# Scaling the odd token tiles by their norm on POOL instead of DVE in a decoder layer

## The chip, the cores and the metric

The kernel runs on one core of a Trainium2 chip. The metric is the device time of one execution in microseconds (us); the median of three runs of the kernel before is 1223.09 us (1221.67 to 1223.1). Engines are named as in the profile: PE multiplies matrices and transposes, DVE is the vector engine, ACT the scalar engine, POOL the general-purpose one (GpSimd), and SP only issues DMA transfers.

## The reference

One layer of a decoder: a pre-normed token mixer (sparse attention with three branches, beside a short gated convolution) and a squared-ReLU MLP, on 1024 tokens of width 1024. What matters here is its very first step:

```
def rms_norm(x, g):
    y = xf * lax.rsqrt(jnp.mean(xf * xf, axis=-1, keepdims=True) + EPS)
    return (y * g.astype(jnp.float32)).astype(x.dtype)
...
h = rms_norm(x, g_mix_norm[l])
z = h @ w_in[l]
```

`z` is then cut into queries, keys and values of the branches, gates and convolution channels. Everything behind it (compressed keys, attention, output projection, MLP) is left as it is by the change.

## The kernel before, in words

**Tiles.** The 1024 tokens are eight tiles `tb` of 128 (one token to a partition). `xts[tb]` (in the profile `xt`, 128x1024 f32) holds a tile. `norm_in(tb)` (line 632) normalizes it: ACT squares it into `junk` and sums into `ss` (line 636); `rsqrt` (line 556) multiplies and adds on DVE (`rs_t`) and raises to the power -1/2 on POOL (`ri`, 128x1); line 639 scales the whole tile in place by `ri`, one number to a token; then PE transposes it in two halves of four 128x128 blocks into a PSUM tile `tp` (line 644). `split_psum` (line 522) takes each half out of PSUM as a high part on ACT (`hTh`) and a rest on DVE (`hTl`); there are three PSUM buffers for `tp`. Tiles 0 to 3 go to `hTh0`/`hTl0`, tiles 4 to 7 to `hTh1`/`hTl1`.

**Products in three terms.** A product in f32 is made of three matmuls (`mm3`, line 526): high by high, high by rest, rest by high. Weights arrive in `w_raw` (two buffers to a shape), and `w_piece` (line 591) makes `w_hi` on ACT and `w_lo` on DVE, four pieces to a chunk of columns. `z_tokens` (line 664) multiplies four pieces with the transposed tokens into `zp`. The first chunk (lines 650 and 748) gives keys and values; `k_norm` and `v_split` finish them on ACT, DVE and POOL (`ksq`, `kri`, `krow`, `vrow`) and SP writes them to DRAM. The raw compressed-branch part goes to DRAM as `kv_d` and comes back as `ch` (line 771) for the compression, whose weights are the pieces `in_w_cmp1`.

**Sums.** `token_sums` (line 692) is a run of 128x512 additions and subtractions on DVE over `hTh` and `hTl` of all eight tiles (`ta`, `tb`, `t1`, `t2`, `t4`), needed later by a fast matrix multiplication.

**Two small loads on POOL's queue.** `gk_bc` and `gq_bc` (line 655), the norm weights of keys and queries spread over all partitions, are loaded by DMAs that POOL issues; one DVE multiplication (line 658) joins them.

**What sets the order.** The code does not run in the order it is written. `Plan` records every operation with what it needs, and `schedule` (line 340) orders them all: at each step the engine that is free first takes the ready operation of the highest priority, by fixed costs for each kind (`cost`, line 292). The resulting order of each engine is written into the program and does not change at run time: an engine that waits for an operand holds all that stands behind it in its row. Almost all operations carry line 268 in the profile, that of the recorder; tile names tell them apart.

Of the kernel before, what the change touches and what calls it, by code (L numbers as in the profile page):

```python
# [13 lines left out]
ALU = mybir.AluOpType  # L14
# [482 lines left out]
def trunk_layer(ctx, tc, x, g_mix_norm, w_in, g_q, g_k, pe_cmp, w_cmp1, b_cmp1, w_cmp2, b_cmp2,  # L497
                conv_w, g_out, w_o, g_ffn_norm, w_up, w_down, out):
    plan = Plan(tc)
    nc = plan.nc  # L500
# [6 lines left out]
    def pool(stack, name, bufs=1, side=None, space=None):  # L507
        kw = {}
        if side is not None:
            kw["side"] = side  # L510
        if space is not None:
            kw["space"] = space
        return stack.enter_context(plan.pool(name=name, bufs=bufs, reuse_waits="tile", **kw))


    def tt(eng, o, a, b, op):
        eng.tensor_tensor(o, a, b, op=op)
# [4 lines left out]
    def split_psum(hi, lo, ps):  # L522
        copy_act(hi, ps)
        tt(nc.vector, lo, ps, hi.bitcast(F32), ALU.subtract)
# [31 lines left out]
    def rsqrt(o, ss, n, scale):  # L556
        t = st.tile([P, n], F32, name="rs_t", tag=f"rs{n}")
        nc.vector.tensor_scalar(t, ss, scale, EPS, op0=ALU.mult, op1=ALU.add)
        nc.gpsimd.tensor_tensor(o, t, mhalf[:, :n], op=ALU.pow)
# [51 lines left out]
    def w_chunk(c0, n, lo_eng=None):  # L611
        return [w_piece(wiv[:, 2 * j:2 * j + 2, c0:c0 + n], [P, 2, n], gcol=G_MIX + 2 * j)
                for j in range(4)]


    with ExitStack() as a:
        xp = pool(a, "xp", bufs=2, side="right")
        xts = [xp.tile([P, D], F32, name="xt", tag="xt", bufs=8) for _ in range(NT)]
        plan.plus = 100.0
        nc.sync.dma_start(xts[0], x2d[0:P])  # L620
        plan.plus = 50.0
        rows = xp.tile([68, P], F32, name="rows", bufs=1)
        nc.sync.dma_start(rows[0:8], g_mix_norm.rearrange("l (k p) -> (l k) p", p=P))
        nc.sync.dma_start(rows[8:16], g_ffn_norm.rearrange("l (k p) -> (l k) p", p=P))
        nc.sync.dma_start(rows[16:24], g_out.rearrange("l (k p) -> (l k) p", p=P))
        nc.sync.dma_start(rows[24:36], conv_w.rearrange("j (k p) -> (j k) p", p=P))
        nc.sync.dma_start(rows[36:68], pe_cmp.rearrange("k (q two) d -> (k q) (two d)", two=2))
        plan.plus = 0.0
        tp = psP.tile([P, 512], F32, name="tp", tag="pt")
        nc.tensor.transpose(tp[:, :68], rows, ident[:68, :68])  # L630
        nc.vector.tensor_copy(cols, tp[:, :68])
        def norm_in(tb):
            xt = xts[tb]
            junk = xp.tile([P, D], BF16, name="junk", tag="junk", bufs=1)
            ss = st.tile([P, 1], F32, name="ss")
            nc.scalar.activation(junk, xt, AF.Square, accum_out=ss)
            ri = st.tile([P, 1], F32, name="ri")
            rsqrt(ri, ss, 1, 1.0 / D)
            nc.vector.tensor_scalar(xt, xt, ri, None, op0=ALU.mult)
            for half in range(2):  # L640
                tp = psP.tile([P, 4, P], F32, name="tp", tag="pt")
                for j in range(4):
                    k = half * 4 + j
                    nc.tensor.transpose(tp[:, j], xt[:, k * P:(k + 1) * P], ident)
                d = (slice(None), slice(half * 4, half * 4 + 4), slice((tb % 4) * P, (tb % 4 + 1) * P))
                split_psum(hTh[tb // 4][d], hTl[tb // 4][d], tp)

        nc.sync.dma_start(xts[1], x2d[P:2 * P])
        norm_in(0)
        kv_pieces = w_chunk(C_KV, 512)  # L650
        for tb in range(2, NT):
            last = nc.sync.dma_start(xts[tb], x2d[tb * P:(tb + 1) * P])
            if tb == 5:
                plan.follow = (last,)
                nc.gpsimd.dma_start(gq_bc, g_q.partition_broadcast(P))
                nc.gpsimd.dma_start(gk_bc, g_k.partition_broadcast(P))
                plan.follow = ()
                tt(nc.vector, gk_bc, gk_bc, gq_bc.unsqueeze(1).to_broadcast([P, 3, HD]), ALU.mult)
                plan.follow = ()
        for tb in range(1, NT):  # L660
            norm_in(tb)
# [60 lines left out]
    with ExitStack() as b1:  # L722
# [129 lines left out]
        for tb, ps in (a for tbs in (QUADS[1], (0,), (1,), (2,), (3,)) for a in z_tokens(pieces, tbs, 512, steps, 1)):  # L852
# [7 lines left out]
            ri = st.tile([P, H], F32, name="qri")  # L860
# [20 lines left out]
        for tb, ps in (a for tbs in (QUADS[1], (0, 1), (2,), (3,)) for a in z_tokens(pieces, tbs, 280)):  # L881
# [6 lines left out]
            for g in range(G):  # L888
                eg = e[:, g * 12:(g + 1) * 12].rearrange("p (i j b) -> p b j i", i=2, b=3)
                nc.vector.tensor_scalar(gates[:, tb, g].rearrange("p b (j i) -> p b j i", j=2), eg, 1.0, 1e20,  # L890
                                        op0=ALU.add, op1=ALU.min)
# [5 lines left out]
    with ExitStack() as b2:  # L897
# [150 lines left out]
        def y_tile(shape, name):  # L1048
            return yp.tile(shape, F32, name=name, tag="y", bufs=6)
# [167 lines left out]
        for it, tb in [*enumerate(ORDER)][6:] + [*enumerate(ORDER)][:6]:  # L1217
            xt = xq.tile([P, D], F32, name="xt") if it >= 6 else y_tile([P, D], f"y{tb}")
            nc.sync.dma_start(xt, x2d[tb * P:(tb + 1) * P])
            t = slice(tb * P, (tb + 1) * P)  # L1220
            for nh in range(2):
# [7 lines left out]
                for c in range(4):  # L1229
# [3 lines left out]
                                               op0=ALU.mult, op1=ALU.add)  # L1233
# [421 lines left out]
    for c in range(NPAIR // CHUNK):  # L1655
# [6 lines left out]
        for p in range(7):  # L1662
# [18 lines left out]
            for j in range(4):  # L1681
# [8 lines left out]
                tb = TH[ih] * 4 + j  # L1690
# [34 lines left out]
```

## Time and profile before

| what | value |
|---|---|
| median of 3 runs | 1223.09 us |
| time of the profiled execution | 1223.71 us |
| its span in the trace | 1221.9 us |
| PE busy in it | 1201.2 us (98%) |
| DVE busy | 918.9 us (75%) |
| ACT busy | 716.1 us (59%) |
| POOL busy | 709.3 us (58%) |
| granted TensorE clock | 1.00 |

The span runs from the first instruction to the last; the 1.8 us by which the execution's time is longer lies around it. Busy shares say how long an engine had an instruction running, not whether it set the pace: where PE issues one 128x512 matmul right behind the other, nothing that another engine does makes it faster. So the places to look at are those where PE waits, and what it waits for.

### The profile page before, as it was taken

The page shows a single profiled execution, that of the slowest core. Times are in us where ns is not written, and L with a number is a line of the kernel's source. Part 1 is how long each engine was busy: PE and PEld are TensorE (multiplying, and loading weights), DVE is VectorE, ACT ScalarE, POOL GpSimd, SP SyncE. Part 2 cuts the span into 40 slices and gives each one's busy share as a digit, 9 for nine tenths or more (in the row PEclk, how much of TensorE's full clock was granted, in tenths as well). Part 3 has the DMA queues.
Part 4 walks back from the last instruction along what each step waited for, and adds up shares of the span by engine and source line. Part 5 has one row for each costly group of instructions (what it writes and reads, how often), then busy time and mean ns, then how long its engine had stood idle before and what let it go on. Part 6 is the DMA issues. An engine that isn't in the chain of part 4 may idle for free.

```text
span 1221.9 us, 18330 instructions
## 1 busy us (share of the span) xinstructions
PE 1201.2 (98%) x5970; PEld 996.9 (82%) x5970; DVE 918.9 (75%) x1784; ACT 716.1 (59%) x1586; POOL 709.3 (58%) x629
## 2 busy tenths in 40 slices
PE   7999999999999999999999999999999999999998
PEld 6878978777878888888788888888888888888887
DVE  6958856684697889988876565656758988888885
ACT  7567855551588878787956555555445444444441
POOL 2544300011345444434759877777888999989971
PEclk9999999999999999999999999999999999999999
DMA  7275631155120101002225544445449545543513
GB/s 247 54 193 180 183 82 52 53 192 187 44 87 36 48 22 36 28 18 70 75 92 178 182 142 151 152 133 181 150 150 394 185 165 165 175 143 121 174 51 138
DMA packets 104215, 156.06 MB, mean 128 GB/s; under 512 B 20212, under 2 KB 58184, under 8 KB 104120
## 3 DMA queue, kind: packets, MB, share of 16 engines
q1 hardware_dynamic: 97976, 147.09, 36.6%
q10 hardware_dynamic: 5376, 5.24, 1.2%
q0 software_dynamic: 768, 2.56, 0.7%
q8 instruction: 47, 0.77, 0.3%
q14 instruction: 48, 0.39, 0.1%
HBM read 106.63 MB, written 48.23 MB: 127 GB/s over the span
## 4 chain that ended last, share of the span: by engine, by line
PE 87%; DVE 5%; ACT 2%; DMA 1%; issue 1%; POOL 1%; SPq 0%; ACTq 0%; DVEq 0%; POOLq 0%
PE X L268 28%; PE Z L268 18%; PE zX L268 5%; PE tp L268 5%; PE ot L268 4%; PE wa L268 4%; PE W L268 4%; PE zp L268 3%; PE wc L268 3%; PE zZ L268 3%; PE zW L268 1%; PE hp L268 1%; DVE w_lo L268 1%; DVE pl L268 1%; PE tpq L268 0%
## 5 line engine op out<-in xcount | busy, mean ns | idle before, releaser
L268 PE MATMUL X<-we,uu 128*128 128x512 f32 x720 | 202.3, 389 | 0.0
L268 PE MATMUL Z<-we,uu 128*128 128x512 f32 x576 | 169.1, 389 | 0.0
L268 PEld LDWEIGHTS X<-we,uu 128*128 128x128 f32 x720 | 135.1, 188 | 28.1
L268 ACT ACTIVATE uu<-ur 128x512 fp32r<-128x512 f32 x108 | 66.5, 630 | 118.9 <-PE Z L268 58.5
L268 PEld LDWEIGHTS Z<-we,uu 128*128 128x128 f32 x576 | 108.1, 188 | 22.5
L268 PE MATMUL tp<-ident,pt 128*128 128x128 f32 x528 | 103.6, 273 | 1.3 <-DVE pl L268 0.7
L268 ACT ACTIVATE pt<-pt,nm 128x640 f32<-128x640 f32 (+7 forms) x128 | 93.7, 735 | 18.9 <-DVE nm L268 18.3
L268 DVE TENSOR_TENSOR y<-X,y 128x512 f32<-128x512 f32 x128 | 86.4, 684 | 20.5 <-PE X L268 20.1
L268 POOL TENSOR_TENSOR d<-d 128x512 f32<-128x512 f32 x64 | 96.2, 1523 | 9.6 <-DVE d L268 7.5
L268 DVE TENSOR_TENSOR pl<-tp,ph 128x512 fp32r<-128x512 f32 (+1 forms) x148 | 94.6, 654 | 7.3 <-ACT ph L268 6.8
L268 ACT ACTIVATE ph<-tp 128x512 fp32r<-128x512 f32 (+1 forms) x148 | 82.2, 576 | 30.0 <-PE tp L268 27.9
L268 DVE TENSOR_TENSOR y<-Z,y 128x512 f32<-128x512 f32 x96 | 65.2, 685 | 27.3 <-PE Z L268 27.1
L268 POOL TENSOR_TENSOR uu<-ur,uu 128x512 fp32r<-128x512 f32 x54 | 82.2, 1527 | 1.1 <-ACT uu L268 0.9
L268 PEld LDWEIGHTS tp<-ident,pt 128*128 128x128 f32 x528 | 68.6, 140 | 14.0 <-POOL pt L268 1.0
L268 DVE TENSOR_TENSOR we<-s,we 128x512 fp32r<-128x512 f32 x42 | 41.1, 978 | 47.6 <-PE Z L268 19.0
L268 ACT ACTIVATE we<-s 128x512 fp32r<-128x512 f32 x55 | 34.7, 631 | 65.3 <-PE Z L268 36.7
L268 ACT ACTIVATE we<-wu 128x512 fp32r<-128x512 f32 x57 | 35.9, 631 | 54.7 <-PE X L268 37.4
L268 POOL TENSOR_TENSOR we<-wd,we 128x512 fp32r<-128x512 f32 x32 | 52.2, 1631 | 25.0 <-ACT we L268 24.5
L268 POOL IOTA d_sw<- 128x640 f32 (+1 forms) x2 | 1.2, 610 | 108.9 <-PE zZ L268 108.9
L268 DVE TENSOR_TENSOR we<-wu,we 128x512 fp32r<-128x512 f32 x38 | 49.5, 1304 | 19.2 <-PE X L268 9.8
L268 PE MATMUL zp<-w_lo,hTh 128*128 128x512 f32 (+1 forms) x192 | 62.2, 364 | 0.1
L268 PE MATMUL zp<-w_hi,hTl 128*128 128x512 f32 (+1 forms) x192 | 61.5, 363 | 0.0
(1334 smaller groups left out, 3733.4 us busy)
## 6 DMA issues: line engine op xcount, KB each, us to landing
u_d<-d SPq DMA_DIRECT2D x112, 256.0 KB, 4.4
ur<-u_d SPq DMA_DIRECT2D x108, 256.0 KB, 2.9
wu<-in_w_up_dram SPq DMA_DIRECT2D x16, 1024.0 KB, 6.2
wd<-in_w_down_dram SPq DMA_DIRECT2D x16, 1024.0 KB, 6.8
xt<-in_x_dram SPq DMA_DIRECT2D x10, 512.0 KB, 5.7
w_raw<-in_w_in_dram SPq DMA_DIRECT2D x8, 512.0 KB, 5.7
w_raw<-in_w_cmp_dram SPq DMA_DIRECT2D x16, 256.0 KB, 2.9
q_d<-qn SPq DMA_DIRECT2D x8, 512.0 KB, 3.5
```

What stands on the lines that cost most here:

```text
L268: node.do.append(lambda: getattr(engine, method)(*[real(x) for x in a], **{k: real(x) for k, x in kw.items()}))
```

## The change

Line 639 chooses the engine by the number of the tile. Tiles 0, 2, 4 and 6 are scaled on DVE as before; tiles 1, 3, 5 and 7 on POOL, behind the power that POOL has computed for that tile. The operation, its operands and its result are the same.

```
             ri = st.tile([P, 1], F32, name="ri")
             rsqrt(ri, ss, 1, 1.0 / D)
-            nc.vector.tensor_scalar(xt, xt, ri, None, op0=ALU.mult)
+            (nc.gpsimd if tb in (1,3,5,7) else nc.vector).tensor_scalar(xt, xt, ri, None, op0=ALU.mult)
             for half in range(2):
```

Since the order is made by the planner, other operations move too, on all engines, from the first token tiles to the end of the compression and the second weight chunk; behind that all rows are as before. Three places follow.

DVE in the first 30 us, before (`xt_165` to `xt_167` are tiles 5 to 7; `w_lo_133` and `w_lo_134` the third and fourth weight piece of the first chunk):

```order
L268 TENSOR_SCALAR rs_t_300<-ss_295 128x1
L268 TENSOR_SCALAR xt_165<-xt_165,ri_272 128x1024
L268 TENSOR_TENSOR hTl1_123<-tp_347,hTh1_124 128x4x128
L268 SCALAR_TENSOR_TENSOR w_lo_133<-w_raw_283,cols_64,w_hi_137 128x512 x2
L268 SCALAR_TENSOR_TENSOR w_lo_134<-w_raw_314,cols_64,w_hi_138 128x512 x2
L268 TENSOR_TENSOR hTl1_123<-tp_364,hTh1_124 128x4x128
L268 TENSOR_SCALAR xt_166<-xt_166,ri_328 128x1024
L268 TENSOR_TENSOR hTl1_123<-tp_375,hTh1_124 128x4x128
L268 TENSOR_SCALAR rs_t_350<-ss_345 128x1
L268 TENSOR_TENSOR hTl1_123<-tp_395,hTh1_124 128x4x128
L268 TENSOR_TENSOR gk_bc_168<-gk_bc_168,gq_bc_169 128x192
```

and in the changed kernel, the same stretch:

```order
L268 TENSOR_SCALAR rs_t_300<-ss_295 128x1
L268 TENSOR_TENSOR gk_bc_168<-gk_bc_168,gq_bc_169 128x192
L268 TENSOR_TENSOR hTl1_123<-tp_348,hTh1_124 128x4x128
L268 SCALAR_TENSOR_TENSOR w_lo_133<-w_raw_283,cols_64,w_hi_137 128x512 x2
L268 TENSOR_TENSOR hTl1_123<-tp_370,hTh1_124 128x4x128
L268 SCALAR_TENSOR_TENSOR w_lo_134<-w_raw_316,cols_64,w_hi_138 128x512 x2
L268 TENSOR_SCALAR xt_166<-xt_166,ri_309 128x1024
L268 TENSOR_SCALAR rs_t_351<-ss_345 128x1
L268 TENSOR_TENSOR hTl1_123<-tp_379,hTh1_124 128x4x128
```

The scaling of tile 5 is gone from DVE, and `gk_bc` has moved from behind the weight pieces to in front of them.

POOL over the same stretch, in the changed kernel (before, its eight `ri` stand there without anything between them but the two DMAs, which come behind the fourth):

```order
L268 TENSOR_TENSOR ri_106<-rs_t_103,mhalf_67 128x1
L268 TENSOR_SCALAR xt_161<-xt_161,ri_106 128x1024
L268 TENSOR_TENSOR ri_107<-rs_t_104,mhalf_67 128x1
L268 TENSOR_TENSOR ri_241<-rs_t_235,mhalf_67 128x1
L268 TENSOR_SCALAR xt_163<-xt_163,ri_241 128x1024
L268 DMA gk_bc_168<-in_g_k_dram 128x192
L268 DMA gq_bc_169<-in_g_q_dram 128x64
L268 TENSOR_TENSOR ri_257<-rs_t_250,mhalf_67 128x1
```

The scaling of tile 3 (`xt_163`) stands ahead of the two DMAs.

SP's queue some 40 us later, before (`ch_818` is the compressed branch read back, `w_raw` in `in_w_cmp1` its weights):

```order
L268 DMA k_d0_193<-krow_791 256x1x64 x2
L268 DMA w_raw_918<-in_w_cmp1_dram 128x2x256
L268 DMA w_raw_932<-in_w_cmp1_dram 128x2x256
L268 DMA ch_818<-kv_d_197 64x1024 x2
L268 DMA v_ds_191<-vrow_875 128x256
```

and in the changed kernel:

```order
L268 DMA k_d0_193<-krow_782 256x1x64 x2
L268 DMA w_raw_919<-in_w_cmp1_dram 128x2x256
L268 DMA ch_806<-kv_d_197 64x1024 x2
L268 DMA w_raw_931<-in_w_cmp1_dram 128x2x256
L268 DMA v_ds_191<-vrow_889 128x256
```

`ch` is issued before the second compression weight instead of behind it. On PE, the eight transposes of `ch` stand seven 128x512 matmuls earlier than before.

## Rows read from the trace of the kernel before

**Rows 1.** Stretches: from:to, length, busy time and count by engine, clock, DMA.

```profile
8.90:30.00 21.10, 21.04 (x110) 17.70 (x110) 19.14 (x38) 18.61 (x36) 5.54 (x9) 1.00 0.73 259
30.00:77.00 47.00, 46.34 (x202) 36.75 (x200) 37.74 (x76) 27.02 (x84) 20.36 (x20) 1.00 0.48 113
```

**Rows 2.** PE's waits over the span: waiter, releaser, us in total, times, longest.

```profile
PE tp L268 <- DVE xt L268: 1.9, 1, 1.9
PE tp L268 <- DMA ch<-kv_d: 1.2, 1, 1.2
...
PE tp L268 <- DVE rs_t L268: 0.6, 1, 0.6
```

**Rows 3.** DVE's groups, first 33 us: count | busy us, mean ns | idle before.

```profile
L268 DVE TENSOR_SCALAR xt<-xt,ri 128x1024 f32<-128x1024 f32 x8 | 6.0, 749 | 1.6 <-POOL ri L268 1.4
```

**Rows 4.** Instructions in order of time, 9 to 13 us: start, length, engine, what.

```profile
9.98 0.75 DVE L268 TENSOR_SCALAR xt<-xt,ri 128x1024 f32<-128x1024 f32 x1 [0.67 <-POOL ri L268]
...
12.99 0.28 PEld L268 LDWEIGHTS zp<-w_lo,hTh 128*128 128x128 f32 x1 [0.19 <-DVE w_lo L268]
```

**Rows 5.** POOL's groups over the span, a two-input and a one-input form.

```profile
L268 POOL TENSOR_TENSOR pt<-pt,rr 128x640 f32<-128x640 f32 x32 | 39.2, 1254 | 0.0
...
L268 POOL CAST Qz<-Qg 64x512 fp32r<-64x512 f32 x16 | 9.7, 608 | 31.9 <-ACT Qg L268 14.8 <-PE s__3927 L268 6.4 <-PE s__6301 L268 2.2
```

**Rows 6.** POOL's instructions in order of time.

```profile
14.40 0.55 POOL L268 TENSOR_TENSOR ri<-rs_t,mhalf 128x1 f32<-128x1 f32 x1 [2.99 <-DVE rs_t L268]
...
15.69 0.56 POOL L268 DMA_DIRECT2D gq_bc<-in_g_q_dram  x1
...
21.46 0.94 POOL L268 TENSOR_TENSOR ri<-rs_t,mhalf 128x1 f32<-128x1 f32 x1 [0.45 <-DVE rs_t L268]
...
34.08 0.46 POOL L268 TENSOR_TENSOR vrow<-z,vrow 128x128 fp32r<-128x128 f32 x1 [6.22 <-ACT vrow L268]
...
42.05 4.88 POOL L268 TENSOR_TENSOR vrow<-z,vrow 128x128 fp32r<-128x128 f32 x1 [2.96 <-issue]
```

**Rows 7.** DVE's instructions in order of time.

```profile
14.78 1.41 DVE L268 SCALAR_TENSOR_TENSOR w_lo<-w_raw,cols,w_hi 128x512 fp32r<-128x512 f32 x2
...
21.16 0.15 DVE L268 TENSOR_SCALAR rs_t<-ss 128x1 f32<-128x1 f32 x1 [0.25 <-ACT junk L268]
21.24 0.75 DVE L268 TENSOR_SCALAR xt<-xt,ri 128x1024 f32<-128x1024 f32 x1
21.91 0.68 DVE L268 TENSOR_TENSOR hTl<-tp,hTh 128x512 fp32r<-128x512 f32 x1
...
27.68 0.35 DVE L268 TENSOR_TENSOR gk_bc<-gk_bc,gq_bc 128x192 f32<-128x192 f32 x1
```

**Rows 8.** DMA issues, first 35 us: queue, count, KB, us to landing.

```profile
gq_bc<-in_g_q_dram POOLq DMA_DIRECT2D x1, 32.0 KB, 4.5
```

**Rows 9.** PE's instructions in order of time.

```profile
23.84 0.39 PE L268 MATMUL zp<-w_lo,hTh 128*128 128x512 f32 x1
...
30.20 1.03 PE L268 MATMUL tp<-ident,xt 128*128 128x128 f32 x8
...
71.01 0.40 PE L268 MATMUL zp<-w_hi,hTl 128*128 128x512 f32 x1
71.46 0.50 PE L268 MATMUL zp<-w_lo,hTh 128*128 128x512 f32 x1
...
75.99 0.40 PE L268 MATMUL zp<-w_lo,hTh 128*128 128x512 f32 x1
77.55 1.06 PE L268 MATMUL tp<-ident,ch 128*128 128x128 f32 x8 [1.17 <-DMA ch<-kv_d]
```

**Rows 10.** SP's issues in order of time.

```profile
70.49 1.99 SPq L268 DMA_DIRECT2D w_raw<-in_w_cmp_dram  x2
```

**Rows 11.** Chain of waits, 60 to 78 us: start, length, what.

```profile
64.16 5.71 DMA w_raw<-in_w_in_dram
...
73.15 4.27 DMA ch<-kv_d
```

More of the change, by code (lines that the diff above doesn't have):

```diff
@@ L638, in norm_in @@
             rsqrt(ri, ss, 1, 1.0 / D)
-            nc.vector.tensor_scalar(xt, xt, ri, None, op0=ALU.mult)
+            (nc.gpsimd if tb in (1,3,5,7) else nc.vector).tensor_scalar(xt, xt, ri, None, op0=ALU.mult)
             for half in range(2):
```

## The prediction

> **What bounds the kernel now.** I read three views: the busy times by stretch, PE's waits, and then single instructions of the first 78 us in order of time, because the change touches only that part and the rows of all engines are as before further on. The busy times [rows 1] show PE busy for 21.04 of 21.10 us up to 30 us and for 46.34 of 47.00 us from there to 77 us. In the second stretch that is not only occupied but paced: 46.34 us over 202 matmuls is 0.23 us each, and a 128x512 matmul comes every 0.23 us wherever PE runs freely. DVE is busy too (37.74 of 47), but it is not what PE stands still for: PE's waits [rows 2] name DVE's first scaling once (1.9 us, tile 0, which the change leaves on DVE), the read-back `ch` once (1.2 us) and one DVE step of the compression (0.6 us). So the most that the change can win lies in the last two and in small gaps, about 2 us of 1223. What it can lose is not capped so: PE runs its row in a fixed order, and a tile or a weight that comes late holds all matmuls behind it.
>
> **What is removed.** DVE loses four of its eight scalings at 749 ns [rows 3], 3.0 us of work. Little of that arrives at PE. The sums on DVE can start only when the last half of tile 7 is transposed and out of PSUM, and these transposes stand in PE's row, at 30.20 us [rows 9]; in the new row six matmuls of 0.23 us less stand ahead of them, 1.4 us, so that they come near 28.8 us plus whatever PE has lost by then. That, and not the 3.0 us, is how much earlier DVE's long run of sums begins.
>
> **What is added.** A scaling of 128x1024 on POOL does not occur in the trace. From above: POOL's two-input operation on 640 columns takes 1254 ns [rows 5], by columns 2.0 us for 1024. From below: DVE's own 0.75 us [rows 3]; a one-input POOL cast of 64x512 takes 0.61 us [rows 5], twice that is 1.2 us with the start counted twice. I take 1.1 us, near the cast, since the scaling also reads one tensor. [...] My value stands on the cast's row.
>
> **Tile 1.** DVE scaled it from 9.98 to 10.73 us, right behind its power [rows 4]. On POOL it starts at the same time and ends at 11.1, so its transposes come 0.3 to 0.4 us later. PE's next fixed point is the first `w_lo` matmul at 12.99, for which PE waited 0.19 us on DVE's `w_lo` [rows 4]; the delay is taken up by that to about 0.1 us: **+0.1**. At 2.0 us it would be +0.8.
>
> **Tile 3 and what stands behind it.** This is the term that costs. Its power ends at 14.95 [rows 6]; DVE then is in two `w_lo` operations with two SBUF inputs, 14.78 to 16.19 [rows 7]. The trace shows that POOL is held in such moments: the same power takes 0.94 instead of 0.55 us when DVE runs a scaling beside it (21.46 against 14.40 in [rows 6], the scaling at 21.24 in [rows 7]), and a `vrow` subtraction takes 4.88 instead of 0.46 us in the thick of DVE's sums [rows 6]. [...]
>
> I take the held value from the rows: start at 16.2, end at 17.3. Its transposes stood at about 18.2 us in PE's row, so tile 3 itself is in time. But POOL issues the two small DMAs behind it. `gq_bc` was issued 0.74 us after the power (15.69 against 14.95, [rows 6]) and landed 4.5 us later [rows 8]; now it lands at 17.3 + 0.74 + 4.5 = 22.5. Before, the DVE multiplication that reads it stood at 27.68 [rows 7], 7 us of cover. In the new row it comes right behind `rs_t` of tile 6, which is done at 21.3 [rows 7]: DVE waits 1.2 us, with one `hTl` and the third weight piece behind it. The first `w_lo` of that piece is ready at 22.5 + 0.35 + 0.6 + 0.7 = 24.2 (the multiplication, an `hTl` at its spacing of 0.6, half of 1.41; [rows 7]). PE had its matmul at 23.84 [rows 9] and now has one matmul less ahead of it: 23.6. **+0.6**. It costs from the point where tile 3's scaling ends later than 16.7, and then one for one.
>
> **Tiles 5 and 7.** Beside them DVE mostly evicts PSUM (`hTl`), and their scalings come earlier than on DVE, because they no longer wait in its row: nothing.
>
> **The weights near 71 us.** Two matmuls stand 0.45 us apart where 0.23 would do (71.01 and 71.46, [rows 9]), behind a weight that landed at 64.16 + 5.71 = 69.87 [rows 11]. DVE frees that weight's buffer after its sums, which end about 0.8 us earlier (1.4 less the 0.6 lost by PE), while PE comes 0.7 later: the gap closes, **-0.2**.
>
> **The read-back at 77 us.** SP issued two compression weights between 70.49 and 72.48 [rows 10], the second held until DVE freed a buffer, and only then `ch`, whose transfer lasts from 73.15 to 77.42 [rows 11]; PE stood still for 1.17 us [rows 9]. Now `ch` goes ahead of the second weight. Issued right behind the first it leaves some 1.6 us earlier, and lands near 75.8; with the 0.8 us by which DVE's and SP's steps before it come earlier, near 75.0. PE reaches the transposes seven matmuls earlier, too: 76.2 - 1.6 + 0.7 - 0.2 = 75.1. So the wait ends between 0.7 and 0, against 1.2: I take **-0.9**, nearer to the end at which SP's row really moves up.
>
> **The later wait of 0.6 us** [rows 2] is behind the compression's DVE chain, which the planner moved up among the queries; it can go, stay or double (the ends -0.6 and +0.6), I take 0.
>
> **The sum.** 0.1 + 0.6 - 0.2 - 0.9 = -0.4 us. Against the profiled execution's 1223.71 us (span 1221.9 and 1.8 around it) that is 1223.3; this execution lies 0.6 above the median of the runs, so against 1223.09 I predict 1222.7 us. Ends of the terms: -0.6 - 0.2 - 1.2 = -2.0 if POOL is never held and every wait goes (1221.1); 0.8 + 1.5 + 0.6 = +2.9 with POOL at 2.0 us, `ch` and the weights unchanged (1226.0).
>
> **Rivals.**
> - *The wait only changes places.* The `gk_bc` stall is paid, and `ch` still comes with the second weight's timing, because SP is held ahead of it by something else, such as the key writes. PE then meets `ch` seven matmuls earlier and waits longer there, but the same matmuls follow at once. +0.7 and nothing back: 1223.8. For it: SP's queue is full of issues that wait for POOL's `kri` and `vrow`. Against: the chain of waits goes through the second weight.
> - *All of it is won.* POOL is not held at tile 3, the multiplication of `gk_bc` finds its data, the waits at 71 and 77 us go: 0.1 - 0.2 - 1.2 = -1.3, 1221.8. Against it: the 0.94 us power.
> - *POOL is starved (slower).* If tile 3's scaling suffers as the `vrow` at 42.05 did, 4.4 us over its free time, it ends at 15.0 + 1.1 + 4.4 = 20.5, `gq_bc` lands at 25.7, and the third weight piece is ready at 27.4: PE loses 3.8 us there, gets back at most 1.1, and is at 1225.8. It decides from an end of about 20 us. Against it: there DVE ran two-input sums back to back for 30 us; here two `w_lo` stand alone, and PSUM evictions follow.
> - That the change does not do what it says is excluded: POOL's row has the four scalings.
>
> **How the numbers follow.** Forecast 0.5, the wait that changes places 0.27, all won 0.14, POOL starved 0.09. A measurement of this kernel tells about 0.2%, 2.4 us, from no change. Only the far end of "all won", with more gaps closing than PE's waits name, reaches that on the fast side: 0.03. Starvation reaches it, and a slow POOL scaling with no gain at `ch` nearly does: 0.08. Within 0.2%: 0.89. The range holds the first three cases with the scatter of the runs (1221.67 to 1223.1) and part of the way to the fourth: 1221.0 to 1225.0.
>
> **What would show it.** Four POOL scalings of about 1.1 us, that of tile 3 beginning near 15.0 and ending near 17.3; DVE idle for about a microsecond before `gk_bc` near 21.3, released by a DMA; PE's `w_lo` matmul of the third piece about 0.6 us late; tile 7's transposes near 29.4; PE's wait for `ch` under 0.7 us. I am wrong if a POOL scaling takes over 2 us, if DVE does not wait at `gk_bc`, or if a new PE wait of over a microsecond shows between 80 and 170 us, where the rows are reordered and I could name no term.

## The result and the profile after

The changed kernel takes 1230.32 us (median of four runs, 1229.76 to 1231.9), the kernel before 1223.09: a ratio of 1.0062, 95% interval 1.0051 to 1.0074. That is 7.2 us slower, outside the range that was given and on the other side of the forecast of 1222.7. The profiled execution took 1229.76 us with a span of 1228.0, against 1223.71 and 1221.9 before. That execution of before lies 0.2 to 1.0 us above the medians of before in the jobs that follow, so a difference between two profiles is smaller than that between two medians by about as much.

The loss is made early. The stretches of the changed kernel, in the columns of [rows 1]:

```profile
8.90:30.00 21.10, 17.61 (x86) 14.28 (x86) 15.31 (x31) 17.73 (x32) 15.45 (x12) 1.00 0.70 234
30.00:77.00 47.00, 47.00 (x212) 38.10 (x211) 38.30 (x76) 25.69 (x73) 25.91 (x21) 1.00 0.44 109
```

From 8.9 to 30 us PE is busy for 17.61 us where it was busy for 21.04, and has done 86 instructions instead of 110. POOL, the fifth pair, is busy for 15.45 us instead of 5.54. From 30 to 77 us PE is fully busy in the changed kernel, and was for 46.34 of 47.00 us before: time lost ahead of that cannot be made up, since next to nothing is left to be filled.

The profile gives 1.00 for the granted clock of all these stretches. But the trace's own record of the clock begins only at 17.63 us (at 14.11 us before); for the time ahead of that, 1.00 is not a measured value. PE's instructions show another pace there. The changed kernel, in the columns of [rows 9]:

```profile
16.53 0.63 PE L268 MATMUL zp<-w_hi,hTl 128*128 128x512 f32 x1
16.96 0.63 PE L268 MATMUL zp<-w_hi,hTh 128*128 128x512 f32 x1
...
19.09 0.39 PE L268 MATMUL zp<-w_hi,hTl 128*128 128x512 f32 x1
19.32 0.40 PE L268 MATMUL zp<-w_hi,hTh 128*128 128x512 f32 x1
```

and the kernel before:

```profile
13.58 0.63 PE L268 MATMUL zp<-w_hi,hTl 128*128 128x512 f32 x1
14.01 0.45 PE L268 MATMUL zp<-w_hi,hTh 128*128 128x512 f32 x1
14.29 0.40 PE L268 MATMUL zp<-w_lo,hTh 128*128 128x512 f32 x1
14.53 0.39 PE L268 MATMUL zp<-w_hi,hTl 128*128 128x512 f32 x1
```

A matmul starts 0.43 us behind the one ahead of it, and later 0.23. 0.43 us is also the spacing in e12 from 74.70 to 78.11 us, where the granted clock is given as 0.50; what clock was granted in the first microseconds no trace shows. Counted from PE's transposes of tile 0, the record begins 5.2 us later before and 9.0 us later in the changed kernel, where PE stood still for 2.0 us in between.

What PE waits for, in the columns of [rows 2], from 0 to 180 us:

```profile
PE tp L268 <- DMA rows<-in_pe_cmp_dram: 6.4, 1, 6.4
PE tp L268 <- POOL xt L268: 3.5, 2, 2.0
PE tp L268 <- DVE xt L268: 1.9, 1, 1.9
PE tp L268 <- DMA ch<-kv_d: 1.3, 1, 1.3
PE hp L268 <- ACT ah L268: 0.9, 1, 0.9
PE tp L268 <- DVE qri L268: 0.7, 1, 0.7
PE hp L268 <- DVE w1l L268: 0.3, 1, 0.3
```

The first line is the load that PE starts with (6.7 us before). The second is new and the largest behind it, 3.5 us in two waits for tiles that POOL scales. `ah` and `w1l` are new as well, 1.2 us together, in the compression. The wait for `ch` is as long as it was, and `qri` stands where `rs_t` stood.

The two waits for POOL, and tile 7, in PE's row:

```profile
12.63 1.12 PE L268 MATMUL tp<-ident,xt 128*128 128x128 f32 x4 [2.00 <-POOL xt L268]
...
26.16 0.66 PE L268 MATMUL tp<-ident,xt 128*128 128x128 f32 x4 [1.50 <-POOL xt L268]
...
33.28 0.97 PE L268 MATMUL tp<-ident,xt 128*128 128x128 f32 x6
```

And POOL's own row, where the answer stands:

```profile
9.72 2.86 POOL L268 TENSOR_SCALAR xt<-xt,ri 128x1024 f32<-128x1024 f32 x1
12.55 0.57 POOL L268 TENSOR_TENSOR ri<-rs_t,mhalf 128x1 f32<-128x1 f32 x1
15.97 0.55 POOL L268 TENSOR_TENSOR ri<-rs_t,mhalf 128x1 f32<-128x1 f32 x1 [2.85 <-DVE rs_t L268]
16.62 3.84 POOL L268 TENSOR_SCALAR xt<-xt,ri 128x1024 f32<-128x1024 f32 x1
20.41 0.76 POOL L268 DMA_DIRECT2D gk_bc<-in_g_k_dram  x1
21.18 0.56 POOL L268 DMA_DIRECT2D gq_bc<-in_g_q_dram  x1
21.74 1.42 POOL L268 TENSOR_TENSOR ri<-rs_t,mhalf 128x1 f32<-128x1 f32 x2
23.26 2.85 POOL L268 TENSOR_SCALAR xt<-xt,ri 128x1024 f32<-128x1024 f32 x1
```

A scaling takes 2.85 us, not 1.1; the fourth is alike (2.86). Tile 2's power (12.55) comes right behind the first scaling, and from 16.62 on POOL goes from one item to the next without a stop. So each scaling delays the powers behind it, and DVE waits for those before its own tiles 2 and 4:

```profile
13.16 0.76 DVE L268 TENSOR_SCALAR xt<-xt,ri 128x1024 f32<-128x1024 f32 x1 [1.81 <-POOL ri L268]
...
22.37 0.75 DVE L268 TENSOR_SCALAR xt<-xt,ri 128x1024 f32<-128x1024 f32 x1 [1.73 <-POOL ri L268]
...
24.24 0.14 DVE L268 TENSOR_SCALAR rs_t<-ss 128x1 f32<-128x1 f32 x1
24.41 0.36 DVE L268 TENSOR_TENSOR gk_bc<-gk_bc,gq_bc 128x192 f32<-128x192 f32 x1
```

`gk_bc`, which was to wait here for its DMA, does not wait: DVE comes to it late enough.

### The profile page after: what moved, and what is told of

The parts are those of the page before. It is cut to its first block, busy times and chain, and to the rows that moved or that the text cites. A ratio compares the mean times of both kernels' runs of the same rounds, so it can differ in the third digit from the quotient of the medians.

```text
span 1228.0 us, 18318 instructions
## 1 busy us (share of the span) xinstructions
PE 1202.5 (98%) x5970; PEld 997.1 (81%) x5970; DVE 915.5 (75%) x1780; ACT 716.4 (58%) x1586; POOL 724.7 (59%) x633
## 4 chain that ended last, share of the span: by engine, by line
PE 87%; DVE 5%; POOL 2%; ACT 2%; DMA 2%; issue 1%; SPq 0%; ACTq 0%; POOLq 0%; DVEq 0%
PE X L268 28%; PE Z L268 18%; PE tp L268 5%; PE zX L268 5%; PE zp L268 5%; PE ot L268 4%; PE wa L268 4%; PE W L268 4%; PE wc L268 3%; PE zZ L268 3%; PE zW L268 1%; PE hp L268 1%; POOL xt L268 1%; DVE w_lo L268 1%; DVE pl L268 1%
## 5 line engine op out<-in xcount | busy, mean ns | idle before, releaser
L268 PE MATMUL zp<-w_hi,hTh 128*128 128x512 f32 (+1 forms) x192 | 62.0, 370 | 0.1
```

The costliest lines, as they stand in the source:

```text
L268: node.do.append(lambda: getattr(engine, method)(*[real(x) for x in a], **{k: real(x) for k, x in kw.items()}))
```

## The experiments

Two theories stood first. **Length**: a POOL scaling takes 2.85 us by itself, so PE gets tiles 1 and 5 late. **Order**: the time is lost by the replanned rows, whoever scales. A third, **port**, has POOL's scaling long only because DVE holds it. The planner's account of an operation and the engine that executes it can be set apart in this program, so that rows and engine change one at a time. All times are medians, with those of before in the same job. The ratio is taken over the executions and not from the two medians, so it can differ from theirs, most of all in e12, where one execution of five took 1229.36 us and the others 1226.17 to 1226.9.

| run | rows | odd tiles scaled by | us | before | ratio, 95% |
|---|---|---|---|---|---|
| change | after | POOL | 1230.32 | 1223.09 | 1.0062 (1.0051 to 1.0074) |
| e1_order_before | before | POOL | 1227.11 | 1223.02 | 1.0030 (1.0018 to 1.0041) |
| e2_order_after | after | DVE | 1225.80 | 1223.02 | 1.0021 (1.0012 to 1.0030) |
| e3_true_cost | a third plan | POOL | 1237.09 | 1223.02 | 1.0108 (1.0092 to 1.0123) |
| e4_broadcast | after | POOL, two-input form | 1227.22 | 1222.70 | 1.0040 (1.0026 to 1.0054) |
| e5_tile1 | before | POOL tile 1, DVE the others | 1226.18 | 1222.70 | 1.0028 (1.0017 to 1.0039) |
| e6_tiles357 | before | POOL 3, 5, 7, DVE 1 | 1224.94 | 1223.51 | 1.0013 (1.0005 to 1.0022) |
| e9_copy | after | nobody; POOL copies | 1224.65 | 1222.70 | 1.0018 (1.0009 to 1.0026) |
| e10_free | before | nobody | 1222.84 | 1222.70 | 1.0001 (0.9992 to 1.0010) |
| e11_plan_short | a fourth plan | DVE | 1225.26 | 1223.51 | 1.0016 (1.0007 to 1.0025) |
| e12_plan_long | a fifth plan | DVE | 1226.25 | 1223.51 | 1.0033 (1.0020 to 1.0046) |

**Rows before, POOL executes (e1_order_before).**

```
-            nc.vector.tensor_scalar(xt, xt, ri, None, op0=ALU.mult)
+            plan.op("DVE", tc.nc.gpsimd if tb in (1, 3, 5, 7) else tc.nc.vector, "tensor_scalar", (xt, xt, ri, None), dict(op0=ALU.mult))
```

> The order of the kernel before on PE, ACT and SP, planned as if DVE scaled all tiles, but POOL executes the scalings of tiles 1, 3, 5 and 7. Theory length (a POOL scaling of 128x1024 by one number to a token takes 2.85 us by itself, and tiles 1 and 5 reach PE late by it): PE still waits about 2.0 us for tile 1 and over 1 us for tile 5, the total is 3 to 5 us above before, 1226 to 1228. Theory order (the rows that the planner made with too short a cost lose the time): nearly nothing is lost, within 1 us of before. Theory port (POOL is long because DVE holds it): the scaling of tile 1, beside which DVE has little to do, is much shorter than the others.

**Rows after, DVE executes (e2_order_after).**

```
-            (nc.gpsimd if tb in (1,3,5,7) else nc.vector).tensor_scalar(xt, xt, ri, None, op0=ALU.mult)
+            plan.op("POOL" if tb in (1,3,5,7) else "DVE", tc.nc.vector, "tensor_scalar", (xt, xt, ri, None), dict(op0=ALU.mult))
```

> The order of the changed kernel on PE, ACT and SP, but DVE executes all eight scalings. Theory length: the loss goes, 1222 to 1225, with no PE wait for a scaled tile but that of tile 0; what remains of waits between 80 and 130 us (3.2 us in the changed kernel against 0.6 before, the wait for ch apart) is what the new order costs by itself, at most 1.5 us. Theory order: 1228 or more.

Both lose: the engine 4.1 us in unchanged rows, the rows 2.8 us with the engine unchanged. Together that is 6.9 of the 7.2 us; by the ratios it is 0.51 of 0.62%, each of the two uncertain by about 0.1%, so the sum fits but is not tight. So neither theory holds alone; length is the larger part, and order costs more than was expected of it. PE's waits for POOL and the neighbours of that line in e1, 0 to 180 us:

```profile
PE tp L268 <- POOL xt L268: 3.6, 2, 2.2
PE tp L268 <- DVE xt L268: 1.9, 1, 1.9
PE tp L268 <- DMA ch<-kv_d: 1.6, 1, 1.6
```

The 3.6 us of waits for POOL are most of the 4.1 us. In e2 there is no wait for POOL; beside the lines for `xt` and `ch` its waits have `ah` (0.9 us) and `qri` (0.7 us), the same two that the changed kernel has. Lining up PE's instructions of the same form and count with those of before, I get these delays (us, starts in the one trace less starts in the other):

| run | tile 0 | 31 to 60 us | 140 to 180 us | end |
|---|---|---|---|---|
| change | -0.3 | 4.6 | 6.1 | 6.0 |
| e1_order_before | -0.9 | 3.7 | 3.8 | 3.5 |
| e2_order_after | -1.0 | -0.5 | 0.7 | 0.8 |
| e9_copy | -0.5 | 0.0 | 1.4 | 1.9 |

The first column is to be taken off the others: it is the load that PE starts with, which came 6.7 us after the start in the trace of before, 6.4 in that of the change and 5.7 in e2's. What the engine costs is lost before 31 us. Of the rows' cost, e2 has lost 0.5 us by then, and 1.2 to 1.5 us are lost between 75 and 95 us (e2, e9 and the change). Counted from tile 0, e2's profile shows 1.9 of the 2.8 us of its median. Its profiled execution was 1.2 us below that median; where the last 0.9 us lie I can't say.

By 31 us e1 has lost 4.6 us from tile 0 on, a microsecond more than its two waits. In e1 and in e5 (below), whose rows are those of before, 0.7 us of it can be read off one by one: four steps from one matmul to the next that took 0.23 to 0.29 us before take 0.43. All four lie ahead of the point where the record of the clock begins, 8.9 and 8.6 us behind tile 0's transposes and not 5.2 as before; that the clock is the reason is not shown. Of the twelve kernels of the table and before, the six in which PE waits for 1.0 to 2.3 us between tile 0 and that point (change 2.0, e1 2.2, e3 2.3, e4 1.0, e5 1.9, e12 1.1) have that beginning 8.6 to 10.2 us behind tile 0, the six others 3.0 to 6.0 us. So a stop of PE at this place seems to cost more than its own length. That is one trace of each, and no run changed the clock alone.

**What POOL's forms take (e8_probe).** Before's kernel, with operations on a tile of their own put ahead of POOL's first work, while DVE has almost nothing to do; its time (1236.21 in one execution) says nothing of the change, since it delays the whole start.

```
+        probe = xp.tile([P, D], F32, name="probe", bufs=1)
...
+        nc.gpsimd.tensor_scalar(probe, probe, mhalf[:, 0:1], None, op0=ALU.mult)
+        nc.gpsimd.tensor_scalar(probe[:, :512], probe[:, :512], mhalf[:, 0:1], None, op0=ALU.mult)
+        nc.gpsimd.tensor_scalar(probe, probe, -2.0, None, op0=ALU.mult)
+        nc.gpsimd.tensor_tensor(probe, probe, mhalf[:, 0:1].to_broadcast([P, D]), op=ALU.mult)
+        nc.gpsimd.tensor_copy(probe, probe)
```

> The kernel before with six extra POOL instructions on a scratch tile at the very start, while DVE is nearly idle: multiplication by one number to a partition on 128x1024 and 128x512, by a constant on 128x1024, by the same number as a two-input operation on 128x1024, and a copy of 128x1024. The output is not touched. Theory length: the first takes 2.8 to 2.9 us with no DVE work beside it, and about half on 512 columns. Theory port: it takes 1.0 to 1.3 us there. The two-input form should take 2.0 us, by the 1254 ns for 640 columns. If the number to a partition is what is slow, the constant takes 1.0 to 1.3 us. The total time is some us longer than before and says nothing.

POOL's row in it, start, length, what:

```profile
1.91 2.85 POOL L268 TENSOR_SCALAR probe<-probe,mhalf 128x1024 f32<-128x1024 f32 x1
...
5.02 1.55 POOL L268 TENSOR_SCALAR probe<-probe,mhalf 128x512 f32<-128x512 f32 x1
...
6.66 2.77 POOL L268 TENSOR_SCALAR probe<-probe 128x1024 f32<-128x1024 f32 x1
...
9.51 1.89 POOL L268 TENSOR_TENSOR probe<-probe,mhalf 128x1024 f32<-128x1024 f32 x1
...
11.89 1.04 POOL L268 COPY probe<-probe 128x1024 f32<-128x1024 f32 x1
```

The 2.85 us are the operation's own: DVE has no instruction running from 0.9 to 5.96 us in that trace, and the first row ends at 4.76. A constant in place of the factor by token changes little (2.77), so the factor isn't it. The copy of the same tile takes 1.04 us, which is what I had taken for the scaling; the two-input multiplication with the factor repeated along the row takes 1.89 and is a third shorter than the one-input form. Port falls for the length of tiles 1, 5 and 7. It adds something at tile 3 only, which took 3.84 us in the changed kernel and 3.25 in e1, with `w_lo` operations of DVE beside it. Those alone don't decide it: tile 5's scaling in e1 (23.47 to 26.32) kept its 2.85 us with `w_lo` operations beside it from 24.39 on.

**Other lengths in the same rows (e9_copy, e4_broadcast).** In the rows of after, POOL runs a shorter operation on the odd tiles: a copy onto itself (e9; the scaling of these tiles is left out), or the two-input multiplication (e4).

```
+            node = (nc.gpsimd if tb in (1,3,5,7) else nc.vector).tensor_scalar(xt, xt, ri, None, op0=ALU.mult)
+            if tb in (1,3,5,7):
+                node.do = [lambda: tc.nc.gpsimd.tensor_copy(xt.real(), xt.real())]
```

> All rows of the changed kernel, but on POOL a copy of the tile onto itself stands in place of each of the four scalings; the scaling of tiles 1, 3, 5 and 7 is left out. The copy took 1.04 us alone, which is the length that the prediction assumed for the scaling. Theory length: only the cost of the new rows is left, as when DVE executes them (1225.8), at most 0.5 more: 1225.5 to 1226.5, with a PE wait for tile 1 under 0.5 us and DVE waiting about a microsecond for gk_bc. Rival (any work of POOL between the powers costs several us, whatever its length): 1228 or more.

```
...
+            if tb in (1,3,5,7):
+                node.do = [lambda: tc.nc.gpsimd.tensor_tensor(xt.real(), xt.real(), ri.real().to_broadcast([P, D]), op=ALU.mult)]
```

> All rows of the changed kernel, but POOL scales tiles 1, 3, 5 and 7 with the two-input multiplication, the factor repeated over the columns, which took 1.89 us alone against 2.85. Theory length: PE's wait for tile 1 falls from 2.0 to about 1.1 us and that for tile 5 from 1.5 to about 0.6, so about 1.8 us of the 7.2 come back: 1228 to 1229. Rival (as above): 1230, as the changed kernel.

One engine, one order of rows, three lengths: 1.04 us gives a ratio of 1.0018, 1.89 gives 1.0040, 2.85 gives 1.0062. At 1.04 us, near my 1.1, PE waits for no tile of POOL's, and the ratio is that of e2, where DVE does the work. So the length alone carries what the engine costs here, by PE's waits and by the pace behind them, and had the estimate of 1.1 us been right, what was left would have been the rows' share. e4 came out 0.8 us and e9 0.9 us below the ranges that I had given them. PE's waits in e4:

```profile
PE tp L268 <- POOL xt L641: 1.3, 2, 1.0
```

In e9, with 1.04 us in place of the scaling, the stall that the prediction had put at `gk_bc` does appear:

```profile
21.63 0.36 DVE L268 TENSOR_TENSOR gk_bc<-gk_bc,gq_bc 128x192 f32<-128x192 f32 x1 [1.10 <-DMA gq_bc<-in_g_q_dram]
```

PE then waits 0.55 us for the `hTl` behind it (at 22.64). Up to 31 us e9 has lost no more than e2 for all that, 0.5 us each from tile 0 on.

**Which tile (e5_tile1, e6_tiles357).** The rows of before, with POOL for tile 1 alone, or for the other three.

```
+            plan.op("DVE", tc.nc.gpsimd if tb in (1,) else tc.nc.vector, "tensor_scalar", (xt, xt, ri, None), dict(op0=ALU.mult))
```

> The order of the kernel before, POOL scales tile 1 alone. Theory length: tile 1 is the one that nothing covers, PE waits about 2.0 us for it, and half of the 4.1 us that all four cost in this order is here: 1225 to 1226. Rival (the tiles cost alike, about 1 us each): 1224.

```
+            plan.op("DVE", tc.nc.gpsimd if tb in (3, 5, 7) else tc.nc.vector, "tensor_scalar", (xt, xt, ri, None), dict(op0=ALU.mult))
```

> The order of the kernel before, POOL scales tiles 3, 5 and 7, DVE tile 1. Theory length: tiles 3 and 7 come in time, tile 5 makes PE wait a good microsecond, as in the run with all four in this order (two waits, 3.6 us together, of which tile 1 is about 2): 1 to 2 us above before, 1224 to 1225. Rival (tile 1 carries all of it): no difference from before.

Tile 1 costs 3.5 us by itself, the other three 1.4; together that is 4.9 against e1's 4.1, a difference that the intervals leave open. In e5 PE waits once for POOL, and longer for `ch`:

```profile
PE tp L268 <- DMA ch<-kv_d: 2.0, 1, 2.0
PE tp L268 <- POOL xt L268: 1.9, 1, 1.9
```

Counted from tile 0, e5's profile loses 3.3 us by 80 us: 1.9 at tile 1, 0.7 by the pace behind it, 0.7 up to the longer wait for `ch`. By the medians it came out 0.2 us above the range that I had given. In e6 the one wait for POOL (1.4 us) is that of tile 5. Tiles 3 and 7 cost nothing at PE in these rows; tile 3 took 2.88 us here, not the 3.84 of the changed kernel.

**What there was to win (e10_free).** The rows of before, the four scalings left out of the program on any engine.

```
+            node = nc.vector.tensor_scalar(xt, xt, ri, None, op0=ALU.mult)
+            if tb in (1,3,5,7):
+                node.do = []
```

> The order of the kernel before, and the scaling of tiles 1, 3, 5 and 7 is left out, so that no engine does it: DVE is relieved of 3.0 us and no tile comes late. This is the most that any engine could win by taking these scalings from DVE in this order. Theory length, with PE as the bound: PE runs without a gap from 15 to 77 us as it is, so at most 1 us is won, 1222 to 1223. Rival (DVE sets the pace up to 70 us, and its relief is worth its 3.0 us): 1220.

A ratio of 1.0001 (0.9992 to 1.0010): taking the 3.0 us from DVE altogether is worth no more than about a microsecond in these rows, and nothing that could be seen. PE's waits up to 180 us are those of [rows 2], to the tenth. However cheaply another engine did these scalings, the kernel of before, in its own order, would gain no more than that by it.

**The planner told the truth, and two other numbers (e3_true_cost, e11_plan_short, e12_plan_long).** In e3 POOL scales the odd tiles and the planner is told 2.85 us for it. In the two others DVE scales all tiles, and the planner is told 0.3 or 1.2 us for the odd ones.

```
+        if method == "tensor_scalar":
+            c = 2.85
```

> The changed kernel with one number of the planner set: a POOL tensor_scalar costs it 2.85 us instead of 0.94. POOL still scales tiles 1, 3, 5 and 7. Theory length: the wait for tile 1 cannot be planned away (PE has nothing else to do then), so 2 us remain, and the wait for tile 5 goes: 1225 to 1227. Theory order: all of the loss was the wrong number, within 1 us of before.

```
+                c = self.told or c
...
+            plan.told = .3 if tb in (1,3,5,7) else None
             nc.vector.tensor_scalar(xt, xt, ri, None, op0=ALU.mult)
+            plan.told = None
```

> DVE scales all eight tiles; only the planner is told 0.3 us for the scalings of tiles 1, 3, 5 and 7 instead of what it assumes for DVE. Instructions are those of before, the rows are planned anew. Theory lottery (any change of one assumed cost gives other rows between the first tiles and 170 us, and these lose or win a few us of their own, as the changed kernel's rows lose 2.8 with DVE executing): a difference of 1 to 4 us from before, of either sign. Rival (the rows of the changed kernel are bad because POOL is in them): within 1 us of before.

> As the run before, with 1.2 us told for the same four scalings. Theory lottery: a difference of 1 to 4 us from before, of either sign, and not the mirror image of the run with 0.3 us. Rival: within 1 us of before.

The true cost makes it worse, 14 us behind before (one of its four executions took 2013.69 us and is left out of the ratio; the others took 1236.33 to 1237.13). PE's waits in e3, 0 to 180 us:

```profile
PE zp L268 <- DVE w_lo L268: 3.8, 2, 2.4
PE tp L268 <- POOL xt L268: 2.3, 1, 2.3
...
PE tp L268 <- DVE rs_t L268: 1.1, 1, 1.1
```

It still waits for one tile of POOL's, and now twice for weights as well. The granted clock falls to 0.50 twice in this trace, for 3.4 us each: at 79.46 us, a microsecond after PE's wait of 2.4 us for a weight, and at 280.84, where PE has waited 2.5 us. The two plans in which no instruction has changed engine lose 0.16% and 0.33%, the second with three waits of PE for `w_hi`, 3.6 us together. That profile is of its slowest execution, 3.1 us above its median: behind a wait of 2.3 us for `w_hi` the clock is at 0.50 from 74.70 to 78.11 us, so it shows more than the median's loss. With e2 that makes three orders that lose between 1.8 and 2.8 us by their medians though nothing else differs. No replanned order that I ran was as good as that of before; whether it is a lucky one among many or the planner is tuned for its costs stays open.

## Why the prediction was wrong, point by point

**The step that failed** is the price of the added operation: "I take 1.1 us, near the cast, since the scaling also reads one tensor." It takes 2.85 us, outside even the upper end of 2.0 that the two-input rows gave. I had bounded a one-input operation from above by a two-input one, as if the number of tensors read set the time. The probe shows the reverse: 1.89 for the two-input form, 2.85 for this one. The cast of [rows 5] is the nearest row to a copy (1.04), not to a scaling. The range ended at 1225.0, below the 1226.0 that my own sum gave for a POOL scaling of 2.0 us.

**Tile 1** was priced at +0.1, with +0.8 at 2.0 us. The mechanism was right, but the size was off and one term was missing. The delay passes to PE less the 0.2 to 0.3 us of slack ahead of `w_lo`. By these steps 2.0 us gives +1.0 (9.98 + 2.0 is 1.25 later than 10.73), not +0.8, and 2.85 us gives some +1.8 to +1.9; PE waited 2.00 us. The 0.7 us by which the matmuls behind that wait stay at the slower pace were in no term, nor were the 0.7 us that e5 loses up to the wait for `ch` (the whole of e5 is 3.2 us in its profile, counted from tile 0, and 3.5 by the medians).

**Tile 3** was to end at 17.3 and to delay `gk_bc` by 1.2 us. It began at 16.62, since its power ended 1.6 us later than before, and ended at 20.46. That POOL would begin only when DVE's two `w_lo` operations are done was my estimate, and no run shows it: this scaling began in the middle of two of them (16.41 to 17.82), and beside `w_lo` operations POOL took 3.84 us here, 3.25 at tile 3 in e1 and 2.85 at tile 5 in e1. I had written that DVE would then lose one for one at `gk_bc`. It did not: `rs_t` of tile 6 was itself late, DVE having waited 1.73 us for the power of tile 4 that stood behind tile 3 and the two DMA issues on POOL; and `gq_bc` landed 3.1 us after its issue, not 4.5. The wait that I had put on the DMA was taken by POOL's row. PE has no wait at this place; tile 3 reaches PE by way of tile 5, as the chain below shows. For the length that I had assumed, the term was right in kind: in e9 DVE waits 1.10 us at 21.63 for that DMA (1.2 near 21.3 in the forecast).

**Tiles 5 and 7** were "nothing". For tile 7 that held. Tile 5 cost 1.5 us. The chain of waits of the changed kernel, 8 to 31 us, shows why; start, length, what:

```profile
16.62 3.84 POOL xt L268
20.46 0.26 POOL gk_bc L268
...
21.18 0.56 POOL gq_bc L268
...
21.74 1.43 POOL ri L268 x2
...
23.26 2.86 POOL xt L268
...
26.16 0.66 PE tp L268 x4
```

From tile 3's scaling to tile 5's transposes the chain is POOL's row alone, 9.5 us without a wait for another engine (0.6 us of it is "issue"). I had costed each scaling against its neighbours on DVE and not added them up on POOL.

**The weights near 71 us**: right, PE's matmuls come every 0.23 us there, though PE's being 4.6 us late could alone have closed that gap. In e2, where PE is not late, there is no gap either. **The read-back**: SP's row did move up, and `ch` was issued ahead of the second weight, at 74.38 where it had been after 72.48:

```profile
73.36 0.56 SPq L268 DMA_DIRECT2D w_raw<-in_w_cmp_dram  x1
74.38 1.15 SPq L268 DMA_DIRECT2D ch<-kv_d  x2
75.57 0.59 SPq L268 DMA_DIRECT2D w_raw<-in_w_cmp_dram  x1
```

Taking off the 4.6 us by which PE is late, that is earlier than before, but PE reaches the transposes seven matmuls earlier too, and still waited 1.29 us. So the -0.9 did not come, also not in e2 (1.5), where POOL is out of it; in e4 and e9, with the same rows, 0.4 us of it did (0.8). This is the rival "the wait only changes places", which was right about this term: SP is held by something else, though not by key writes. `ch` can be read only when the write of `kv_d` to DRAM has landed, at 74.30 us in the changed kernel and 69.86 in e2, where SP waited 1.0 us for it; the issue follows 0.1 us behind. So once the weight is out of the way that write sets the time, and I had not looked at it.

**The rows from 77 us on** I had priced at 0, between -0.6 and +0.6, for the one wait that I knew. Another came. ACT's rows in the changed kernel:

```profile
89.52 0.63 ACT L268 ACTIVATE w1h<-w_raw 128x512 fp32r<-128x512 f32 x1 [1.01 <-DMA w_raw<-in_w_cmp_dram]
...
90.36 0.61 ACT L268 ACTIVATE ah<-araw 128x512 fp32r<-128x512 f32 x1
```

`ah` stands behind a weight piece in ACT's row, that piece waits for its transfer, and PE waits 0.9 us for `ah`; e2 has the same wait. That reordered rows could cost 2.8 us without any operation being longer was in none of my cases. No new wait of over a microsecond stands behind 80 us, so the sign that I had named for this did not show, and the loss came in smaller pieces.

**The rivals.** "POOL is starved" had the sign and the place where it begins, but not the mechanism. Its end of tile 3, 20.5 us, came true (20.46) for another reason: a start 1.6 us later, 2.85 us of the operation's own and 1.0 us more at this place, not 4.4 of holding. Its price at `gk_bc` did not arise; the loss arose at tiles 1 and 5. "All of it is won" fell with PE's 2.00 us at tile 1. What was written as the sign of error, a POOL scaling over 2 us and no wait at `gk_bc`, is what the profile showed.

## What to carry to other kernels

An operation that does not occur on an engine in the trace has no upper bound from another form on that engine, however much simpler it looks (here 2.85 us, where the two-input rows gave 2.0 as the upper end): where the forecast hangs on it, time it by itself first or let the range hold a far higher price. Add up what a moved operation does to the row of the engine that takes it before looking for collisions: POOL computed the power that every tile waits for, so each 2.85 us on it came ahead of the next tile. And where a planner sets the order, price the reordering apart from the operation: here 4.1 us came from the longer instruction and 2.8 from the order alone, and relief of an engine that PE does not wait for was worth nothing (e10, 1.0001). And here a stop of PE in the first microseconds went with a slower pace of the matmuls behind it, 0.7 us in e1 and e5 beside the stop itself; it is to be priced with that, not by its length alone.

## What the runs showed of the hardware that I had not expected

- On POOL a one-input scaling of 128x1024 f32 is slower than a two-input multiplication by a repeated factor: 2.85 against 1.89 us; by a constant 2.77, of 512 columns 1.55, a copy 1.04 (all e8_probe).
- Operations of POOL and DVE that ran beside each other were longer in some places, on either engine. Beside `w_lo` operations on DVE the scaling of tile 3 took 3.84 us instead of 2.85 (changed kernel), and the copy 1.51 instead of 1.04 (e9). Beside that of tile 3 in e6, two `w_lo` operations took 2.65 us instead of 1.41. Beside POOL's copy in the probe, a DVE scaling took 1.50 instead of 0.75:

```profile
11.97 1.50 DVE L268 TENSOR_SCALAR xt<-xt,ri 128x1024 f32<-128x1024 f32 x1 [3.82 <-POOL ri L268]
```

Tile 5 in e1 shows nothing of the kind: its scaling (2.85 us) and four `w_lo` operations (2.74 us, as long as in the kernel before) ran side by side for 1.9 us without either becoming longer, and why is open.

- PE's 128x512 matmuls start every 0.43 us until 17.4 us in the changed kernel and until 14.0 us before, although the profile gives a granted clock of 1.00 for these stretches: its record of the clock begins at 17.63 and 14.11 us. Behind PE's waits of 2.3 to 2.5 us in e3 and e12, one trace of each, the granted clock was 0.50 for 3.4 us.
